# Softmax over 16,384 rows of 512: the two late loads go from GpSimd's DMA queue to SyncE's, between the stores

## The chip, the cores and the metric

The kernel runs on one core of a Trainium2 chip. The metric is the device time of one execution in microseconds (us), taken as the median of several runs. One further execution was profiled; every row of a profile below comes from such an execution.

## The reference

```python
x = randn(16, 1024, 512)  # float32
x_scaled = x / 2.0
x_max = max(x_scaled, axis=-1)
exp_x = exp(x_scaled - x_max)
out = exp_x / sum(exp_x, axis=-1)      # float32, same shape
```

It is a softmax over the last axis with a temperature of 2. There are 16,384 rows of 512 numbers: 33.55 MB are read and 33.55 MB written.

## The kernel before

The rows are dealt to the 128 partitions, so each partition has 128 rows of 512 numbers (2 KB each). They are cut into ten tiles of 3, 5, 15, 15, 15, 15, 15, 15, 15 and 15 rows per partition (`TILES`), numbered 0 to 9. A tile of 15 rows is 3,840 KB: 30 KB from each partition, which is one DMA packet of 30,720 bytes per partition and eight such packets for each of the 16 DMA engines.

On-chip memory holds 98 rows per partition (`arena`), so tiles 0 to 7 have places of their own, and tiles 8 and 9 reuse places: tile 8 lies over tiles 0, 1 and 2, and tile 9 over tiles 2 and 3. These two are the late loads (`LATE`). A late load may only be issued when the stores of what lies under it have landed: `s_home[8]` counts the landings of stores 0, 1 and 2, and `s_home[9]` counts that of store 3. (For tile 9 the wait for tile 8 has been passed already, which covers store 2.)

The work of each engine, in its own order:

- SyncE (SP) issues load 0 at the start and later all ten stores, in the order of the tiles (L214, L215). It waits first until tile 2 has been multiplied (`FIRST`), then issues stores 0, 1 and 2, and each further one as its tile's multiplies are done (`s_mul`, L138).
- ScalarE (ACT) issues loads 1 to 7 at the start, and then goes through the tiles row by row: one exponential of 512 numbers for each row, which also leaves the row's sum in `stats` (L206 and L274). Rows are counted in chunks of 5; before each chunk ACT takes a token (`s_go`, L142), which TensorE's queue hands on when the tile's load has landed. No maximum is subtracted.
- VectorE (DVE) takes 15 rows at a time (5 in the last tile): reciprocal of the sums (L168), then a multiply of the rows in place (L171).
- GpSimd (POOL) issues loads 8 and 9 (L178 to L181). It waits first until the exponentials have come to row 83 (`TURN`), and for each late load for its `s_home`. After that it clamps all sums for a test whether they are in a sound range (L182, once all exponentials are done).
- The test goes on over DVE (L186), a one-number matmul (L198) and a flag (L190). With the flag set, a slow version with the maximum, in the functions `vector`, `scalar` and `gpsimd`, is skipped, as it is with these data.
- SP waits at the end until the second-last store (`s_near`) and all others (`s_end`, L260) have landed.

DMAs of SP, ACT and GpSimd go into one queue each; the 16 DMA engines serve all three queues. The profile names them by number and tells the kinds apart: those of SP and ACT are `hardware_dynamic`, that of GpSimd is `software_dynamic`.

Of the kernel before, what the change touches and what calls it, by code (L numbers as in the profile page):

```python
# [13 lines left out]
LATE = {8: (0, 1, 2), 9: (3,)}  # L14
# [4 lines left out]

SPREAD = 1  # L20

TURN = 83

FIRST = 2

# [5 lines left out]
def kernel(  # L31
# [5 lines left out]
    nc = tc.nc  # L37
# [30 lines left out]
    def dram(ap, t):  # L68
        b, r, _ = tiles[t]
        return ap[b * P : (b + r) * P].rearrange("(p r) d -> p r d", r=r)  # L70

    def sb(t):
        _, r, at = tiles[t]
        return arena[:, at : at + r, :]
# [3 lines left out]
    starts = [sum(sizes[:k]) for k in range(len(sizes))]  # L78
# [15 lines left out]
    s_home = {t: nc.alloc_semaphore(f"s_home{t}") for t in LATE}  # L94
    s_near = nc.alloc_semaphore("s_near")
    s_end = nc.alloc_semaphore("s_end")
    s_exp = nc.alloc_semaphore("s_exp")
# [17 lines left out]
    def load(eng, t):  # L115
        r = tiles[t][1]
        parts = [(0, P, 0, r)]
        if t == SPREAD:
            parts = [(0, P, 0, r - 1), (0, 126, r - 1, r), (126, P, r - 1, r)]
        for p, q, lo, hi in parts:  # L120
            eng.dma_start(  # L121
                out=sb(t)[p:q, lo:hi], in_=dram(xf, t)[p:q, lo:hi]
            ).then_inc(ld[t], 16)
# [6 lines left out]
    def landings(ts):  # L130
        return 16 * len(list(ts))
# [5 lines left out]
    def store(eng, t):  # L137
        eng.wait_ge(s_mul, upto[t])  # L138
        eng.dma_start(out=dram(of, t), in_=sb(t)).then_inc(sem_of.get(t, s_end), 16)

    def take(eng, sem, n):
        eng.wait_ge(sem, n).then_inc(sem, -n)  # L142

    def rounds(eng, body):


        i = eng.alloc_register("general")
        eng.wait_ge(s_near, 16)
        eng.wait_ge(s_flag, 1)
        eng.reg_load(i, flag[0:1, 0:1])  # L150
        with eng.While(lambda: eng.snap(i, min_val=0, max_val=1) < 1):
            body()
            eng.reg_add(i, i, 1)
# [9 lines left out]
    def program():  # L163

        for j, ks in enumerate(pairs):
            b, c = starts[ks[0]], sum(sizes[k] for k in ks)
            a = b % ARENA
            nc.vector.reciprocal(  # L168
                out=recip[:, b : b + c], in_=stats[:, b : b + c]
            )._wait_ge(s_exp, ks[-1] + 1).then_inc(s_rec, 1)  # L170
            nc.vector.tensor_mul(  # L171
                out=arena[:, a : a + c],
                in0=arena[:, a : a + c],
                in1=recip[:, b : b + c].unsqueeze(2).to_broadcast([P, c, D]),
            )._wait_ge(s_rec, j + 1).then_inc(s_mul, 1)

        nc.gpsimd.memset(ones[:, :], 1.0).then_inc(s_ones, 1)  # L177
        nc.gpsimd.wait_ge(s_exp, starts.index(TURN))  # L178
        for t, us in LATE.items():
            nc.gpsimd.wait_ge(s_home[t], landings(us))  # L180
            load(nc.gpsimd, t)  # L181
        nc.gpsimd.tensor_scalar(  # L182
            out=inside[:, :], in0=stats[:, :], scalar1=LO, scalar2=HI,
            op0=Alu.max, op1=Alu.min,
        )._wait_ge(s_exp, len(sizes)).then_inc(s_cnt, 1)
        nc.vector.scalar_tensor_tensor(  # L186
            out=inside[:, :], in0=inside[:, :], scalar=1.0, in1=stats[:, :],
            op0=Alu.mult, op1=Alu.is_equal, accum_out=count[:, :],
        )._wait_ge(s_cnt, 1).then_inc(s_cnt, 1)
        nc.vector.tensor_scalar(  # L190
            out=flag[:, :], in0=total[:, :], scalar1=float(N), scalar2=None, op0=Alu.is_ge,
        )._wait_ge(s_tot, 1).then_inc(s_flag, 1)


        for t in range(len(tiles)):
            nc.tensor.wait_ge(ld[t], 48 if t == SPREAD else 16).then_inc(s_go, owner.count(t))
        nc.tensor.wait_ge(s_ones, 1)
        nc.tensor.matmul(  # L198
            total[:, :], lhsT=count[:, :], rhs=ones[:, :], start=True, stop=True
        )._wait_ge(s_cnt, 2).then_inc(s_tot, 1)  # L200

        nc.scalar.preload_act_table(Exp)  # L202
        for k, c in enumerate(HEAD):
            take(nc.scalar, s_go, 1)
            for b in range(starts[k], starts[k] + c):
                ins = nc.scalar.activation(  # L206
                    out=arena[:, b], in_=arena[:, b], func=Exp, scale=0.5,
                    accum_out=stats[:, b : b + 1],
                )
            ins.then_inc(s_exp, 1)  # L210
        exponentials(straight, n_rows)

        nc.sync.wait_ge(s_mul, upto[FIRST])
        for t in range(len(tiles)):  # L214
            store(nc.sync, t)  # L215

        x_g = xf.rearrange("(t p r) d -> t p r d", p=P, r=G)
        o_g = of.rearrange("(t p r) d -> t p r d", p=P, r=G)  # L220
        data = arena[:, 0:G]

        def vector():
            for i in range(n_rows // G):
                nc.vector.reduce_max(
                    out=g_max[:, :], in_=data, axis=mybir.AxisListType.X, negate=True
                )._wait_ge(g_go, i + 1).then_inc(g_top, 1)
                nc.vector.reduce_sum(
                    out=g_sum[:, :], in_=data, axis=mybir.AxisListType.X
                )._wait_ge(g_exp, i + 1).then_inc(g_add, 1)  # L230
                nc.vector.reciprocal(
                    out=g_sum[:, :], in_=g_sum[:, :]
                )._wait_ge(g_add, i + 1).then_inc(g_rec, 1)

        def scalar():
            for i in range(n_rows // G):
                nc.scalar.activation(out=data, in_=data, func=Exp, scale=0.5)._wait_ge(
                    g_sub, i + 1
                ).then_inc(g_exp, 1)

        def gpsimd():
            nc.gpsimd.wait_ge(s_end, at_end)
            for i in range(n_rows // G):
                nc.gpsimd.dma_start(out=data, in_=x_g[i]).then_inc(g_ld, 16)
                nc.gpsimd.wait_ge(g_ld, 16 * (i + 1)).then_inc(g_go, 1)
                nc.gpsimd.tensor_add(
                    out=data, in0=data, in1=g_max[:, :].unsqueeze(2).to_broadcast([P, G, D])
                )._wait_ge(g_top, i + 1).then_inc(g_sub, 1)
                nc.gpsimd.tensor_mul(
                    out=data, in0=data, in1=g_sum[:, :].unsqueeze(2).to_broadcast([P, G, D])  # L250
                )._wait_ge(g_rec, i + 1).then_inc(g_mul, 1)
                nc.gpsimd.wait_ge(g_mul, i + 1)
                nc.gpsimd.dma_start(out=o_g[i], in_=data).then_inc(g_st, 16)
                nc.gpsimd.wait_ge(g_st, 16 * (i + 1))

        rounds(nc.vector, vector)
        rounds(nc.scalar, scalar)
        rounds(nc.gpsimd, gpsimd)
        nc.sync.wait_ge(s_near, 16)
        nc.sync.wait_ge(s_end, at_end)  # L260

    def exponentials(first, end):
        row = nc.scalar.alloc_register(f"row{first}")
        nc.scalar.reg_mov(row, first)
        with nc.scalar.While(lambda: nc.scalar.snap(row, min_val=first, max_val=end) < end):
            now = nc.scalar.snap(row, min_val=first, max_val=end - E)
            take(nc.scalar, s_go, 1)
            at = nc.s_assert_within(
                now % ARENA, 0, ARENA - E,
                skip_runtime_bounds_check_because="no chunk reaches over the arena's end",  # L270
            )
            for r in range(E):
                data = arena[:, r : ARENA - E + 1 + r][:, bass.ds(at, 1)]
                ins = nc.scalar.activation(  # L274
                    out=data, in_=data, func=Exp, scale=0.5,
                    accum_out=stats[:, r : n_rows - E + 1 + r][:, bass.ds(now, 1)],
                )
            ins.then_inc(s_exp, 1)
            nc.scalar.reg_add(row, row, E)
# [12 lines left out]
    nc.switch_body(here, parent=None, valid_engines=[i.engine for i in jumps])  # L292
    loads()
    program()


# [28 lines left out]
```

## Time and profile before

| what | value |
|---|---|
| median of 3 runs | 159.78 us (159.69 to 159.83) |
| profiled execution, whole | 160.85 us |
| profiled execution, span of the page | 159.50 us |
| moved over the span | 67.11 MB, mean 421 GB/s |
| busy: DVE, ACT, POOL, PE | 73.2, 80.4, 2.2, 0.2 us |
| SP's issues: stores 0 to 2, 3, 4 | from 35.04, 44.2, 53.4 us |
| SP's issues: stores 5, 6, 7, 8, 9 | 63.57, 75.25, 91.18, 119.81, 132.57 us |
| GpSimd's issues: loads 8, 9 | 77.63, 89.73 us |
| ACT resumes for tiles 8, 9 | 102.02, 120.19 us |
| last landing (store 9) | 159.46 us |

The page counts an engine as busy only while it computes; issuing a DMA is no busy time for SP and ACT. Times are from the start of the span, which is SP's issue of load 0. The profiled execution is 1.07 us longer than the median of the runs without a profile. The lines of the profile on which the working rests stand in the prediction.

### The profile page before, as it was taken

What the parts mean: (1) busy time and instruction counts of PE and PEld (TensorE: products, weight loads), DVE (VectorE), ACT (ScalarE), POOL (GpSimd) and SP (SyncE); (2) the same over time, 40 slices, a digit from 0 to 9 for tenths busy, and PEclk for the clock granted to TensorE, in tenths of its full rate; (3) what the DMA queues carried; (4) which work ended last, traced back from release to release, by engine and by line L of the source; (5) the groups of instructions that cost most, each with busy time, mean ns of one, the idle gap of its engine ahead of it and who ended that gap; (6) DMA issues with size and microseconds to landing.
All of it is one profiled execution on the core that took longest, in us unless ns stands there. A gap on an engine that the chain in (4) does not pass through costs nothing. (4 is left out here: it accounts for less than half of the span.)

```text
span 159.5 us, 658 instructions
## 1 busy us (share of the span) xinstructions
PE 0.2 (0%) x2; PEld 0.1 (0%) x2; DVE 73.2 (46%) x27; ACT 80.4 (50%) x257; POOL 2.2 (1%) x8
## 2 busy tenths in 40 slices
PE   0000000000000000000000000000000000000000
PEld 0000000000000000000000000000000000000000
DVE  0047003989989599298029800000990993000000
ACT  0590699999979859705970000499008940000000
POOL 0000000000000000000100100000000010000000
DMA  7999999999999899999999999999999999999993
GB/s 276 411 455 401 462 408 455 408 455 393 444 461 443 344 434 465 401 462 408 455 424 439 416 447 431 431 447 416 455 408 470 393 470 393 462 401 470 393 470 154
DMA packets 3024, 67.11 MB, mean 421 GB/s; under 512 B 336, under 2 KB 336, under 8 KB 720
## 3 DMA queue, kind: packets, MB, share of 16 engines
q1 hardware_dynamic: 1584, 34.34, 50.2%
q10 hardware_dynamic: 1152, 24.90, 36.8%
q0 software_dynamic: 288, 7.86, 11.5%
HBM read 33.55 MB, written 33.55 MB: 421 GB/s over the span
## 5 line engine op out<-in xcount | busy, mean ns | idle before, releaser
L274 ACT ACTIVATE arena<-arena x125 | 76.6, 615 | 43.4 <-ACTq L142 43.4
L171 DVE TENSOR_TENSOR arena<-arena,recip 128x7680 f32<-128x7680 f32 (+2 forms) x12 | 70.2, 5846 | 0.4
L168 DVE RECIPROCAL recip<-stats 128x15 f32<-128x15 f32 (+2 forms) x12 | 2.7, 224 | 59.3 <-ACT arena L274 50.3
L274 ACT ACTIVATION_READ_ACCUMULATOR arena<-arena x125 | 23.4, 187 | 0.0
L202 ACT ACT_TABLE_LOAD x1 | 1.3, 1283 | 5.7 <-issue 5.7
L121 POOL DMA_DIRECT2D arena<-in_x_dram x2 | 1.3, 632 | 86.3 <-DMA out_dram<-arena 86.3
L206 ACT ACTIVATE arena<-arena 128x512 f32<-128x512 f32 x3 | 1.9, 618 | 0.0
L182 POOL TENSOR_SCALAR inside<-stats 128x128 f32<-128x128 f32 x1 | 0.6, 631 | 39.3 <-ACT arena L274 39.3
L206 ACT ACTIVATION_READ_ACCUMULATOR arena<-arena 128x1 f32 x3 | 0.6, 186 | 0.0
L198 PE MATMUL total<-ones,count 128*1 128x1 f32 x2 | 0.2, 164 | 132.8 <-DVE inside L186 132.8
L186 DVE SCALAR_TENSOR_TENSOR inside<-inside,stats 128x128 f32<-128x128 f32 x1 | 0.3, 285 | 0.0
L190 DVE TENSOR_SCALAR flag<-total 1x1 int32<-1x1 f32 x1 | 0.1, 146 | 0.3 <-PE total L198 0.3
L198 PEld LDWEIGHTS total<-ones,count 128*1 128x1 f32 x2 | 0.1, 80 | 132.8 <-DVE inside L186 132.8
L177 POOL MEMSET ones<- 128x1 f32 x1 | 0.1, 99 | 2.2 <-POOLq L39 2.2
L309 POOL MEMSET const-float32-0.0<- 128x1 f32 x1 | 0.1, 105 | 0.2 <-issue 0.2
L309 POOL MEMSET const-bfloat16-1.0<- 128x1 bf16 x1 | 0.1, 108 | 0.0
L309 POOL MEMSET const-uint8-127<- 128x1 uint8 x1 | 0.1, 108 | 0.0
L309 POOL MEMSET const-float32-1.0<- 128x1 f32 x1 | 0.1, 105 | 0.0
L186 DVE DVE_READ_ACCUMULATOR inside<-inside,stats 128x1 f32 x1 | 0.1, 84 | 0.0
## 6 DMA issues: line engine op xcount, KB each, us to landing
out_dram<-arena SPq DMA_DIRECT2D x8, 3840.0 KB, 47.7
arena<-in_x_dram ACTq DMA_DIRECT2D x6, 3840.0 KB, 36.5
arena<-in_x_dram POOLq DMA_DIRECT2D x2, 3840.0 KB, 27.1
out_dram<-arena SPq DMA_DIRECT2D x1, 1280.0 KB, 27.9
arena<-in_x_dram ACTq DMA_DIRECT2D x1, 1024.0 KB
arena<-in_x_dram SPq DMA_DIRECT2D x1, 768.0 KB, 5.6
out_dram<-arena SPq DMA_DIRECT2D x1, 768.0 KB, 15.2
arena<-in_x_dram ACTq DMA_DIRECT2D x1, 252.0 KB
```

The source lines that it names most:

```text
L121: eng.dma_start(out=sb(t)[p:q, lo:hi], in_=dram(xf, t)[p:q, lo:hi]).then_inc(ld[t], 16)
L168: nc.vector.reciprocal(out=recip[:, b : b + c], in_=stats[:, b : b + c])._wait_ge(s_exp, ks[-1] + 1).then_inc(s_rec, 1)
L171: nc.vector.tensor_mul(out=arena[:, a : a + c], in0=arena[:, a : a + c], in1=recip[:, b : b + c].unsqueeze(2).to_broadcast([P, c, D]),)._w ...
L177: nc.gpsimd.memset(ones[:, :], 1.0).then_inc(s_ones, 1)
L182: nc.gpsimd.tensor_scalar(out=inside[:, :], in0=stats[:, :], scalar1=LO, scalar2=HI, op0=Alu.max, op1=Alu.min,)._wait_ge(s_exp, len(sizes) ...
L186: nc.vector.scalar_tensor_tensor(out=inside[:, :], in0=inside[:, :], scalar=1.0, in1=stats[:, :], op0=Alu.mult, op1=Alu.is_equal, accum_ou ...
L190: nc.vector.tensor_scalar(out=flag[:, :], in0=total[:, :], scalar1=float(N), scalar2=None, op0=Alu.is_ge,)._wait_ge(s_tot, 1).then_inc(s_f ...
L198: nc.tensor.matmul(total[:, :], lhsT=count[:, :], rhs=ones[:, :], start=True, stop=True)._wait_ge(s_cnt, 2).then_inc(s_tot, 1)
L202: nc.scalar.preload_act_table(Exp)
L206: ins = nc.scalar.activation(out=arena[:, b], in_=arena[:, b], func=Exp, scale=0.5, accum_out=stats[:, b : b + 1],)
L274: ins = nc.scalar.activation(out=data, in_=data, func=Exp, scale=0.5, accum_out=stats[:, r : n_rows - E + 1 + r][:, bass.ds(now, 1)],)
L309: nc = _bacc.Bacc("TRN2", target_bir_lowering=False, num_devices=1)
```

## The change

GpSimd no longer issues the two late loads and no longer waits for row 83 or for the `s_home` semaphores. SP issues them in its chain of stores: load 8 after store 3 and ahead of store 4, and load 9 after store 4 and ahead of store 5, each after a wait for the same count of its `s_home` as before. Nothing else differs: the same transfers in the same sizes, the same places in `arena`, the same arithmetic.

```diff
-TURN = 83
+AHEAD = {4: 8, 5: 9}
...
         nc.gpsimd.memset(ones[:, :], 1.0).then_inc(s_ones, 1)
-        nc.gpsimd.wait_ge(s_exp, starts.index(TURN))
-        for t, us in LATE.items():
-            nc.gpsimd.wait_ge(s_home[t], landings(us))
-            load(nc.gpsimd, t)
         nc.gpsimd.tensor_scalar(
...
         nc.sync.wait_ge(s_mul, upto[FIRST])
         for t in range(len(tiles)):
+            if t in AHEAD:
+                late = AHEAD[t]
+                nc.sync.wait_ge(s_home[late], landings(LATE[late]))
+                load(nc.sync, late)
             store(nc.sync, t)
```

On SP's queue the order of the transfers becomes: load 0, stores 0, 1, 2, 3, load 8, store 4, load 9, stores 5, 6, 7, 8, 9.

## The prediction

> **What bounds the kernel now.** I read the slices and the DMA queues of the page first, then what the DMA queues' sequencer SP waits for, then the DMA traffic by stretches, then the last 4 us slice by slice, and last the packet records of the trace (start, duration, queue and bytes of each packet, which the views only sum).
>
> The page's slices and queues:
>
> ```profile
> DMA  7999999999999899999999999999999999999993
> ...
> q1 hardware_dynamic: 1584, 34.34, 50.2%
> q10 hardware_dynamic: 1152, 24.90, 36.8%
> q0 software_dynamic: 288, 7.86, 11.5%
> ```
>
> The 16 DMA engines are full from the second slice to the last but one, while DVE (46%) and ACT (50%) have free time. By size, q1 is SP's queue (all stores and load 0), q10 ACT's (loads 1 to 7) and q0 GpSimd's (loads 8 and 9, 7.86 MB). The chain of waits on the page ends with DVE's flag at 133.2 us, 26 us before the span does: it follows engines, and what ends last here is a transfer. SP's own waits say so:
>
> ```profile
> SPq L139 <- DVE arena L171: 118.2, 8, 28.3
> SPq L260 <- DMA out_dram<-arena: 26.5, 1, 26.5
> ```
>
> After its last issue SP waits 26.5 us (L260) for stores already queued. The stores have a backlog, so compute time and the order among transfers do not set the end; bytes per DMA engine, and time lost by one engine, do. The stretches:
>
> ```profile
> core 0: us, PE busy (x) PEld busy (x) DVE busy (x) ACT busy (x) POOL busy (x), PEclk, DMA share, GB/s
> 73.00:82.00 9.00, 0.00 (x0) 0.00 (x0) 2.22 (x1) 8.61 (x29) 0.73 (x1) 1.00 1.01 437
> ...
> 92.00:117.00 25.00, 0.00 (x0) 0.00 (x0) 5.62 (x2) 9.29 (x30) 0.00 (x0) 1.00 1.00 433
> 119.00:156.00 37.00, 0.19 (x2) 0.09 (x2) 10.18 (x10) 9.29 (x30) 0.63 (x1) 1.00 1.00 431
> ```
>
> SP's queue alone (73 to 82, 119 to 156) and SP's beside GpSimd's (92 to 117) move the same 431 to 437 GB/s. Last, DMA from 156 to 160 us in slices of 0.1 us:
>
> ```profile
> DMA  0079999077000000000700000000000000000000
> GB/s 0 0 307 922 1843 614 614 0 307 307 0 0 0 0 0 0 0 0 0 307 0 0 0 0 0 0 0 0 0 0 0 0 0 0 0 0 0 0 0 0
> ```
>
> A packet counts where it begins. Fifteen engines begin their last packet between 156.2 and 157.0; the single 307 in the slice at 157.9 is the last packet of one engine, late by itself. That engine sets the end. Call it A.
>
> A can be followed back packet by packet, each start on the end before it. Its completion for store 2 is at 76.65 us, against a median of 75.85 over the 16: 0.80 late. For store 9 it is at 159.11 against 157.57: 1.54 late. The added 0.74 is one packet. Nearly every 30,720-byte packet takes 1,138 ns on every queue; the one that A begins at 89.14 on q0 takes 1,875, 737 more. Of the 1,201 such packets that begin after 72 us only three take over 1,250 ns: this one, and two of another engine B (87.01 and 89.58 us; 1,441 and 1,516). All three are on GpSimd's queue. GpSimd issues load 9 meanwhile:
>
> ```profile
> 77.63 0.73 POOL L121 DMA_DIRECT2D arena<-in_x_dram  x1 [74.88 <-DMA out_dram<-arena]
> 89.73 0.54 POOL L121 DMA_DIRECT2D arena<-in_x_dram  x1 [11.37 <-DMA out_dram<-arena]
> ```
>
> A's and B's second long packets both contain 89.73 to 90.27. At the first issue (77.63) no q0 packet was moving yet, and none on q1 was slowed.
>
> **The change, part by part.** *Removed from GpSimd:* two issues (0.73 and 0.54 us) and their waits. GpSimd then waits for the last exponential (129.57 now), which is off the path: nothing gained.
>
> *Added to SP:* two waits and two issues of 0.33 to 0.44 us (the ten store issues; load 0's took 0.38). The first wait, for stores 0 to 2 landed, ends at 77.00 as before, since everything up to there is unchanged. Behind it stands store 4, which is issued at 53.4 now (end of its multiply) and would be at about 77.4 + 0.33. Behind the second, for store 3, stand stores 5 and 6. What covers both waits is the queue: at 77.0 store 3 has begun (its 8 packets per engine take 8 x 1.135 = 9.1 us), so it runs to 75.85 + 9.1 = 84.9, and load 8 is queued 7.5 us before that. From issue to first packet with full engines took 3.55 us (store 0: 35.04 to 38.59), so 4 us of cover remain; without the cover, that 3.55 would be a hole in the DMA stream. The second wait ends when A lands store 3, 85.7 + 0.35 = 86.1, with load 8 and store 4 still queued until 103: 17 us of cover. Both waits cost nothing.
>
> *Order of the transfers:* in one queue, at 9.1 us each: store 3 to 84.9, load 8 to 94.0, store 4 to 103.1, load 9 to 112.2, stores 5, 6, 7 to 139.4, store 8 to 148.5, store 9 to 157.6. Now, two queues share the engines packet by packet, and the loads land at 101.7 and 119.8; then at 95.2 and 113.3 (A's lag and 0.35 us added). Exponentials and multiplies follow sooner: store 8 is issued 18.1 us after its load lands now (101.7 to 119.8), so at 113.3, 26 us before its turn; store 9 12.8 us after (119.8 to 132.6), so at 126.1, 22 us before its turn. The queue does not run dry; these gains go nowhere.
>
> *Turns between reading and writing inside one queue* (store 3, load 8, store 4, load 9, store 5: four). The trace has none. Nearest row: A alternates a q1 store with a q0 load packet from 91 to 118 us, nearly every packet, with no gap and 1,138 ns each. Farthest: load 0 on idle engines, 0.63 us from the end of its issue (0.38) to its first packet (1.01). A gain is excluded, as neither queue has gaps. So 0 to 4 x 0.63 = 2.5 us; I take 0, since the near row is the same engine doing the same turns.
>
> *The long packets of q0.* They end with the queue, unless they belong to the moment instead. Bounds for the end: 0, and all of A's lag, 1.54. I take 0.74: from 119 to 156 us, SP's queue alone, no packet is over 1,250 ns. The other 0.80 of the lag stays, as it was there at 76.65; 0.60 of it is a packet of 1,738 ns at 61.3 on q10, beside q1. The Trainium skill (DMA: Bandwidth & Descriptors, "Latency and other measured facts") notes that DMA engines 7 and 15 are usually slower and guesses, for GpSimd's software path alone, at contention on the ports of its descriptor rings. The trace has two slow engines on q0 as it says, but A's lag of 61.3 us came without GpSimd; were the rule the whole of it, a hardware-only schedule would end at the median engine, and the sum would be 159.78 - 1.54 = 158.24.
>
> **Sum.** In the profiled execution (span 159.50, whole 160.85) A would end 0.74 earlier: span 158.76. The median of the runs is 159.78, 1.07 below the profiled whole; taking the same difference off it, 159.78 - 0.74 = 159.04, 0.46% less. From 0.2% (0.32 us) this kernel can be told from no change: its runs lie within 159.69 and 159.83.
>
> **Rivals.**
>
> *Same bytes, same time (0.23).* The delay at 89 us is of the moment: all but two engines had packets of 1.2 to 1.55 us at 54.5 without GpSimd, and A had its own at 61.3. Then A loses as much elsewhere, or the unprofiled runs never lost it. Against: q1 alone shows no such packet for 37 us. It gives 159.6 to 159.9, middle 159.78. The Trainium skill (same page, "Issuing engines are not separate DMA queues") has this as its rule: who issues changes only the issue time, as all queues run on the same 16 engines; by it the time stays at 159.78, and the 431 to 437 GB/s above agree with it.
>
> *Turns cost (0.14), slower.* Where SP's queue goes from a store to a load, the engine waits for the first bytes of the new read. Two turns at 0.63 us give 159.04 + 1.26 = 160.3, four give 161.6. Against: A's gapless alternation; for: there the packets came from two queues. It decides from (0.74 + 0.32)/4 = 0.27 us per turn.
>
> *The queue runs dry (0.05).* If load 8 reached the engines later than store 3's end, up to 3.55 us per wait would be lost: 159.04 + 3.55 = 162.6 for one. It needs 4 us more from issue to first packet than any SP issue here showed.
>
> That the change does not do what it says (loads later than now) would need a wait that ends later; both end at or before today's 77.0 and 89.4, and at 22 us of slack a late load shows in no time. I give it nothing of its own.
>
> **How the numbers follow.** The forecast has 0.58: 159.04, by itself 158.2 (all of A's lag gone) to 159.45. With the same-time case and the two-turn price the range is 158.2 to 160.3. Faster 0.58, same 0.23, slower 0.14 + 0.05 = 0.19.
>
> **What would show it.** Right: no q0; q1 1,872 packets and 42.2 MB; load 8 landed near 95 and load 9 near 113; ACT resuming near 95.5 and 113.6; SP's last issue near 126 and its wait at L260 about 32 us; no packet over 1,250 ns after 72 us; A about 0.8 behind the median at the end. A lag of 1.5 with the last store would show the second case; gaps or long packets between 85 and 112 us where load follows store the third; a dip in the DMA slices at 85 or 103 the fourth. A median over 159.46 makes the forecast wrong.

## The result, and the profile after

The changed kernel is slower: 161.49 us median of 6 runs (160.74 to 162.32), against 159.81 us for 6 runs of the kernel before beside them. The ratio is 1.0106, with a 95% interval of 1.0072 to 1.0140. Three later measurements, each in a batch of its own, put it at 1.0046 (1.0008 to 1.0083), 1.0049 (1.0018 to 1.0081) and 1.0046 (1.0007 to 1.0084). These ratios are of means. By the medians the changed kernel is slower by 1.68 us in the first batch and by 0.74, 0.27 and 0.30 us in the later ones: its six runs of the first batch were all over 160.7 us, while 16 of the 35 later ones were under 160.3. The sign held each time; the size depends on the batch, from 0.5 to 1.1% by the means.

The page after, slices and queues:

```profile
DMA  7998989899999899999999999999999999999994
...
q1 hardware_dynamic: 1872, 42.21, 61.9%
q10 hardware_dynamic: 1152, 24.90, 36.8%
```

GpSimd's queue is gone and its 288 packets are on q1. The DMA engines are as full as before. In the view by stretches (columns as in the prediction; the last two are the DMA share and GB/s):

```profile
73.00:82.00 9.00, 0.00 (x0) 0.00 (x0) 2.27 (x1) 8.47 (x27) 0.00 (x0) 1.00 1.01 437
...
119.00:156.00 37.00, 0.19 (x2) 0.09 (x2) 8.19 (x8) 4.85 (x16) 0.63 (x1) 1.00 1.01 435
```

The kernel before had 437 and 431 GB/s there. Over the whole stretch from 73 to 156 us it moved 432 GB/s and the changed kernel 430. SP's own waits:

```profile
SPq L139 <- DVE arena L171: 71.0, 5, 24.1
SPq L121 <- DMA out_dram<-arena: 40.1, 2, 31.9
SPq L260 <- DMA out_dram<-arena: 32.3, 1, 32.3
```

The second row is new, SP's two waits for landed stores. The third is the wait after the last issue: 32.3 us in place of 26.5. ACT's starts on the late tiles, in the timeline:

```profile
95.35 0.63 ACT L274 ACTIVATE arena<-arena  x1 [12.53 <-ACTq L142]
...
114.56 0.63 ACT L274 ACTIVATE arena<-arena  x1 [9.91 <-ACTq L142]
```

Both late loads land sooner than before (ACT resumed at 102.02 and 120.19 us there). So everything ahead of the last transfers got earlier or stayed, and the kernel got slower. The end, DMA from 156 to 161 us in slices of 0.125 us, a packet counted where it begins:

```profile
DMA  9559999559550000050000000000000000000000
GB/s 492 246 246 492 983 492 492 246 246 492 246 246 0 0 0 0 0 246 0 0 0 0 0 0 0 0 0 0 0 0 0 0 0 0 0 0 0 0 0 0
```

The same view of the kernel before:

```profile
DMA  0099955500000005000000000000000000000000
GB/s 0 0 983 1475 737 246 246 246 0 0 0 0 0 0 0 246 0 0 0 0 0 0 0 0 0 0 0 0 0 0 0 0 0 0 0 0 0 0 0 0
```

Before, 15 engines begin their last packets within 0.65 us, and one follows 1.05 us later. After, the 15 are spread over 0.97 us (the first slices hold packets before the last, too), and one follows 0.70 us later, at 158.1. By the packet records, the last engine ends 1.37 us behind the median of the 16 (157.89 and 159.26), and the median itself came 0.31 us later than before (157.58). How far the last engine is behind the median of the 16 when a transfer lands is called its lag below.

The records also show where that arose. After 72 us the changed kernel has 18 packets of 30,720 bytes over 1,250 ns, the kernel before three. Such packets are called long or stretched below. They stand in the late loads, above all in the last packets of load 8 (from 92.8 us) and of load 9 (from 110.8 us), up to 1,758 ns in place of 1,138. One can see it in the DMA view from 108 to 116 us (slices of 0.2 us). First the changed kernel's profile of 161.00 us, then its fourth one, of 160.00 us:

```profile
GB/s 154 154 154 922 768 461 0 154 307 1229 614 154 154 0 614 922 614 154 154 0 154 768 768 154 307 307 307 768 461 461 307 154 768 614 154 614 154 154 922 614
```

```profile
GB/s 0 0 0 1382 768 307 0 0 154 1690 461 154 0 0 614 1536 307 0 0 0 922 1229 307 0 0 0 1382 768 307 0 0 461 1536 307 154 0 0 922 1229 307
```

The engines begin their packets in a bunch every 1.13 us. In the second row the bunch stays narrow past load 9's end (about 112.2); in the first it frays from 111 us on and never closes again, since from there each engine has the same work left.

Those two profiles are of one kernel, and that is needed to read every number below: executions of one kernel differ in how late the last engine is. Over all batches, 77 of 115 runs of the kernel before were under 160.3 us, 33 between 160.3 and 161.0, and 5 over 161.0. Of the changed kernel 16 of 41 were under 160.3, 6 between, and 19 over 161.0. In all 18 profiles the whole time is 1.73 to 1.89 us more than the end of the last engine's last packet, so the time follows the last engine.

### The profile page after: what moved, and what is told of

The parts are those of the page before. It is cut to its first block, busy times and chain, and to the rows that moved or that the text cites. A ratio compares the mean times of both kernels' runs of the same rounds, so it can differ in the third digit from the quotient of the medians.

```text
span 159.6 us, 657 instructions
## 1 busy us (share of the span) xinstructions
PE 0.2 (0%) x2; PEld 0.1 (0%) x2; DVE 73.2 (46%) x27; ACT 80.4 (50%) x257; POOL 0.9 (1%) x6
## 2 busy tenths in 40 slices
DMA packets 3024, 67.11 MB, mean 420 GB/s; under 512 B 336, under 2 KB 336, under 8 KB 720
```

## The experiments

The theory was that turns, that is, changes from load to store or back inside SP's queue, stretch load packets, unevenly over the engines, and that the worst engine is the time. The rivals were that SP's queue is short at its new waits, that GpSimd's software queue suits the loads better than a hardware queue, that reading and writing in stretches is slower than side by side, and that chance made the difference. Since the runs scatter, the numbers below are means, each against the kernel before in the same batch. Batches ran on different chips, so differences are compared, not times.

**Does the packet that the prediction counted on come back?** The kernel before, once more:

> The kernel before, unchanged, for a second profile. If the 1,875 ns packet of GpSimd's queue at 89 us comes with every execution, it is there again, with a span near 159.5 us and a last engine 1.5 us behind the median. If it belonged to that one execution (the median of the runs, 159.8, less the 1.35 us outside the span would be a span of 158.4), the last engine is about 0.5 to 0.8 us behind and the span is near 158.4.

This execution took 160.54 us. The 1,875 ns packet was not there. One engine had three others on q0 (88.57, 93.56 and 107.35 us; 1,573, 1,314 and 1,520 ns) and ended 1.26 us behind the median. So that packet belonged to that one execution, but long packets on q0 as such did not. The two profiles of the kernel before, 160.85 and 160.54 us, are both from the upper third of its runs (median here 159.86).

**No turns: late loads on ACT's queue.**

```diff
-        nc.gpsimd.wait_ge(s_exp, starts.index(TURN))
-        for t, us in LATE.items():
-            nc.gpsimd.wait_ge(s_home[t], landings(us))
-            load(nc.gpsimd, t)
...
-        exponentials(straight, n_rows)
+        exponentials(straight, ARENA)
+        for t, us in LATE.items():
+            nc.scalar.wait_ge(s_home[t], landings(us))
+            load(nc.scalar, t)
+        exponentials(ARENA, n_rows)
```

> Late loads issued by ScalarE on its own hardware queue, when it is through with tile 7 (about 83 us) and store 3 has landed (about 89 us). Theory (turns): what costs is a queue that goes from load to store, which stretches the last packet of each late load by 0.05 to 0.6 us, another amount on each engine. With the loads in a queue of their own no queue turns: 159.5 to 160.0 us, like before, and no packet over 1.25 us at the ends of loads 8 and 9. Rival (hardware queues): late loads cost more when a hardware queue carries them: 161.0 to 162.0. Rival (short queue: at the waits SP's queue holds only what remains of store 3): here the stores are issued as before, so 159.8 too.

160.29 us mean against 159.95 (ratio 1.0023, 1.0004 to 1.0042): near the kernel before, well below the change's first 161.5. And beside the changed kernel in one batch:

> Late loads on ACT's hardware queue, beside the stores on SP's: no turns. Theory (turns): mean 0.5 us or more below the changed kernel, within 0.4 us of the kernel before. Rival (hardware queues are worse for late loads than GpSimd's): like the changed kernel.

160.24 against 160.04 before (ratio 1.0013, 0.9989 to 1.0037) and 160.61 for the changed kernel: 0.37 below the change where 0.5 was expected, and by itself within the scatter of these 11 and 11 runs (about 0.6 us either way). Over both batches one of 23 runs was over 161.0 us, of the changed kernel 19 of 41. That speaks against the hardware queue as the cost. But a late engine is found here too: in this profile (160.73 us) it ends 1.33 us behind the median, after long packets on q10 beside the stores.

**Two turns: both loads together, ahead of store 5.**

```diff
-AHEAD = {4: 8, 5: 9}
+AHEAD = {5: (8, 9)}
...
-            if t in AHEAD:
-                late = AHEAD[t]
+            for late in AHEAD.get(t, ()):
```

> Both late loads on SP's queue, one right behind the other, between store 4 and store 5: two turns in place of four, one of them from load to store (at the end of load 9). Theory (turns): half of the 1.7 us of the change or somewhat more, since the worst engine counts: 160.4 to 160.9 us; long packets at the end of load 9, none at the end of load 8. Rival (short queue): store 4 is issued early again, so the queue is as deep as before: 159.8. Rival (no mixing: reading and writing in stretches of their own is slower than side by side): the stretches are as long in sum, 161.5.

160.38 against 159.95 (1.0031, 1.0007 to 1.0056). The mean is just below what the theory gave (160.4 to 160.9), the median of 160.15 further below. The one profile fell on a run of 159.77 us; it has one long packet (1,518 ns at 96.3 us, early in load 8) and none at the end of load 9, where the theory had put them. Ahead of store 4 (`AHEAD = {4: (8, 9)}`), where SP's queue is short:

> Both late loads together ahead of store 4: two turns, and a short queue, since store 4 is only issued after store 3 has landed (about 86 us). Theory (turns): like the pair ahead of store 5, 159.9 to 160.5 us. Rival (short queue): like the change or slower, 161.0 to 162.0.

> Both late loads together ahead of store 4: two turns. Theory (turns): between the kernel before and the changed one, mean 0.4 to 1.0 us below the changed one; few runs over 161.0. Rival (short queue): like the changed one or slower.

160.26 against 160.36 (ratio 1.0000, 0.9971 to 1.0030), and 160.26 against 160.04 (1.0022, 0.9998 to 1.0047). With a short queue the pair is no slower than with a long one, and both times below the changed kernel (161.08 and 160.61 in the same batches; only the first of these differences is clear of the scatter). Its profiles, of 159.77 and 160.15 us, have five and four long packets at the end of load 9 (1,253 to 1,422 ns), and yet the last engine ends only 0.30 and 0.59 us behind the median. So long packets alone do not cost time; they do where they make the last engine later.

**Four turns, later: the long queue.**

```diff
-AHEAD = {4: 8, 5: 9}
+AHEAD = {5: 8, 6: 9}
```

> Load 8 ahead of store 5 and load 9 ahead of store 6, one place later than in the change. Store 4 is issued at 53.4 us again, so SP's queue holds stores 3 and 4 at the first wait and is never shorter than one whole store; the number of turns stays at four. Theory (turns): as slow as the change, 161.0 to 161.9 us, with stretched last packets of load 8 near 102 us and load 9 near 120 us. Rival (short queue): like before, 159.7 to 160.1.

160.71 against 160.36 (1.0031, 0.9990 to 1.0071, so not clear of no change), and 161.08 for the changed kernel there. Seven of 12 runs were at 159.92 to 160.05, five at 161.30 to 162.12. Five runs that late go against the short queue; seven at 160.0 go against the theory as it was worded, with 161.0 for all. In this kernel's profile ACT resumes for the late tiles at 104.23 and 122.64 us, later than in the kernel before, so the earlier landing of the loads in the change does not explain its late runs either.

**Four turns with smaller packets.** Each late load in parts of 8 and 7 rows:

```diff
+        if t in LATE:
+            parts = [(0, P, 0, 8), (0, P, 8, r)]
```

> Each late load in parts of 8 and 7 rows as in the kernel with eight turns, but the two parts of a load together: load 8 ahead of store 4, load 9 ahead of store 5, so four turns and the same packet sizes as with eight. Theory (turns): like the change, 161.0 to 161.9 us. Rival (more and smaller packets make the cost of the kernel with eight turns): like that one, 162.0 to 162.7.

160.80 against 160.36 (1.0025, 0.9989 to 1.0061): as the changed kernel or less.

**Eight turns: the same parts, each ahead of a store of its own.**

```diff
-AHEAD = {4: 8, 5: 9}
+AHEAD = {4: (8, 0), 5: (8, 1), 6: (9, 0), 7: (9, 1)}
```

> Each late load in two parts of 8 and 7 rows, with the four parts ahead of stores 4, 5, 6 and 7 on SP's queue: eight turns in place of four, four of them from load to store. Theory (turns): the cost of the change grows to 1.4 to 2 times: 162.2 to 163.2 us, and long packets stand at the ends of all four parts. Rival (short queue): the second wait and later stores are as covered as in the changed kernel: 161.5. Rival (no mixing): shorter stretches come closer to mixing: 161.0 to 161.5.

> Eight turns once more, beside four and sixteen on the same chip. Theory (turns): 1 us or more above the changed kernel, 161.8 to 162.8 us, with no run near 160. Rival (the five runs of the first time were chance): like the changed kernel.

162.36 against 159.95 and 161.87 against 160.16, both within what was expected; 11 runs, the lowest 161.04. That is 2.41 and 1.71 us above the kernel before. With the same packet sizes and four turns it was 0.44 us, in another batch, so the turns add more than a microsecond. Beside the changed kernel in the second batch (160.73) the 1.14 us are clear of the scatter. In the first profile the last engine is 0.23 us behind the median ahead of load 8, 0.84 after its first part, 1.27 after its second, and 2.26 at the end of load 9.

**Sixteen turns, and the same parts in four.** The late loads in parts of 4, 4, 4 and 3 rows, stores 4 and 5 in thirds, store 6 in halves. `ORDER` goes part by part, one of a load and one of a store, or puts all parts of load 8 ahead of store 4 and all of load 9 ahead of store 5:

```diff
+CUT = {8: (0, 4, 8, 12, 15), 9: (0, 4, 8, 12, 15), 4: (0, 5, 10, 15), 5: (0, 5, 10, 15), 6: (0, 8, 15)}
...
-        for t in range(len(tiles)):
+        for what, t, part in ORDER:
```

> Late loads in parts of 4, 4, 4 and 3 rows, stores 4 and 5 in thirds and store 6 in halves, one part of a load and one of a store in turn on SP's queue: sixteen turns in place of four. Theory (turns): slower than with eight, 163 to 166 us. Rival (no mixing: reading and writing in stretches is what costs): finer stretches come close to two queues side by side, 159.8 to 160.8.

> The same parts as with sixteen turns, but in the order of the change: all parts of load 8, of store 4, of load 9, of the later stores. Four turns, the same packet sizes. Theory (turns): like the changed kernel, mean 160.4 to 161.6 us. Rival (smaller packets cost): as with sixteen turns.

> The changed kernel, four turns, as the measure of this batch. Theory (turns): mean 0.3 to 1.7 us above the kernel before, runs from 159.9 to 162.3.

The means are 161.71 for sixteen turns, 161.23 for the same parts in four, 160.73 for the changed kernel and 160.16 for the kernel before. Finer interleaving did not bring SP's queue near two queues side by side, so the lack of mixing is not the cause. Nor did sixteen turns cost more than eight (161.87 here): the theory's 163 to 166 was wrong. Small parts may cost as well: with four turns each, 161.23 is 0.50 us over the changed kernel, and the sixteen turns are another 0.48 us over that, but neither step is clear of the scatter (about 0.7 and 0.6 us either way). The records show where the lag stops growing, not why. With sixteen turns it goes from 0.27 us at store 2 to 0.51 at store 3 and then by the parts of load 8 to 0.97, 1.63 and 2.22 us, and there it stays through all of load 9's turns. The step at store 3 is a store packet of 1,400 ns, the last ahead of load 8. With four it jumps from 1.06 to 2.33 at the end of load 8 and stays. In no profile did it end over 2.33. The tail with sixteen turns, again from 156 us in slices of 0.125:

```profile
DMA  5500059905050005000000000500000000000000
GB/s 246 246 0 0 0 246 983 2212 0 246 0 246 0 0 0 246 0 0 0 0 0 0 0 0 0 246 0 0 0 0 0 0 0 0 0 0 0 0 0 0
```

Fifteen engines begin their last packets within 0.7 us; the last one does so in the slice at 159.1, and ends 2.22 us behind the median, about two packets.

**The changed kernel again, and no late loads at all.**

> The changed kernel once more, beside the variants on one chip, and a second profile of it. Theory (turns): 161.0 to 161.9 us; the last packet of load 8 (near 93 us) and of load 9 (near 111 us) is stretched again on most engines, and the last engine is over 1.2 us behind the median at the end. If the stretched packets of the first profile were chance, they are missing here while the time is the same.

161.08 against 160.36; profile 161.02 us, last engine 1.60 behind. Its lag grows from 0.45 to 0.95 at the end of load 8 and to 1.60 at the end of load 9: the long packets are there again, but only on a few engines (five over 1,250 ns), not on most.

> The changed kernel beside the others of this batch: four turns on SP's queue. Theory (turns): the slowest of the batch, mean 161.0 to 161.6 us, with most runs over 160.5; stretched packets only in loads 8 and 9 after 72 us. Rival (chance of the batch): mean within 0.3 us of the kernel before.

160.61 against 160.04. This time the profile fell on a run of 159.90 us: no packet over 1,250 ns in the late loads, last engine 0.47 behind. Over its four profiles the changed kernel has 18, five, none and one long packets in the late loads at 161.00, 161.02, 159.90 and 160.00 us: time and stretch come and go together here. Six of its 11 runs were under 160.5, so "most over 160.5" was wrong.

> Left out: loads 8 and 9. Tiles 8 and 9 are computed on what lies in their place once the stores under it have landed; all ten stores stay. Loads 1 to 7 still run beside stores 0 to 2, but after 72 us only stores are in the queues. The time falls by 2 x 9.1 = 18.2 us, to 141.3 to 141.6. Theory (only load packets that have stores beside or behind them are stretched, and one late engine is the time): no run more than 0.3 us above the fastest, the last engine within 0.6 us of the median. Rival (late engines come from loads 5 to 7 beside stores 0 to 2, or from the stores): runs a whole microsecond above the fastest are as frequent as in the kernel before in this same batch.

```diff
-        for t, us in LATE.items():
-            nc.gpsimd.wait_ge(s_home[t], landings(us))
-            load(nc.gpsimd, t)
...
+            if t in LATE:
+                nc.tensor.wait_ge(s_home[t], landings(LATE[t])).then_inc(s_go, owner.count(t))
```

141.85 us mean of 5 runs, 141.65 to 142.31. The tail from 138 us in slices of 0.125:

```profile
DMA  5999090500000000000000000000000000000000
GB/s 246 737 1720 492 0 492 0 246 0 0 0 0 0 0 0 0 0 0 0 0 0 0 0 0 0 0 0 0 0 0 0 0 0 0 0 0 0 0 0 0
```

After 72 us, with only stores in the queues, no packet was over 1,250 ns and the last engine's lag stayed at 0.69 to 0.70 us from store 2 to the end. That lag had come with loads 5 to 7 beside stores 0 and 1 (1.98 us at store 1). One run was 0.66 above the fastest, twice what was expected, so the late loads are the larger source of lag but not the only one.

**All runs by the number of turns.** Runs over 161.0 us, a time that is rare in the kernel before:

| turns in SP's queue | kernels | runs over 161.0 us |
|---|---|---|
| none | kernel before; late loads on ACT's queue | 5 of 115; 1 of 23 |
| two | pair ahead of store 5; ahead of store 4 | 3 of 12; 3 of 24 |
| four | the change; later; in parts of 8 and 7; in four parts | 19 of 41; 5 of 12; 4 of 12; 5 of 12 |
| eight | parts of 8 and 7 rows | 11 of 11 |
| sixteen | parts of 3 to 8 rows | 5 of 6 |

The chips differ (four of the five late runs of the kernel before are of one batch), but the share rises with the turns up to eight.

## Why the prediction was wrong

- **"Long packets of q0" (-0.74 us) failed first.** The term was read from one packet of one execution and taken off the median of others. That execution was 160.85 us, the median 159.78, and two runs in three of the kernel before are under 160.3. The 1.07 us between the two was taken as a fixed difference between profile and runs. The records put it down to the late engine: every profile takes 1.73 to 1.89 us beyond the end of its last engine. No profile of the kernel before fell on a run near 159.8 us; in the six profiles of other kernels at 159.77 to 160.05 us the last engine is only 0.29 to 0.56 us behind the median. So at 159.8 us a gain of 0.74 was not there to be had. The rival "same time" had named this case ("the unprofiled runs never lost it").
- **"Turns" at 0 (of 0 to 2.5 us) failed second, and weighs more.** Of the 2.45 us between the forecast 159.04 and the measured 161.49, 0.77 is the gain that did not come and 1.68 the cost of the change, which this term had at nothing. The nearest row, one engine alternating a store and a load from two queues without a gap, did not carry over to one queue. With the change's four turns the mean rose by 0.57 to 1.70 us in four batches. The rival's mechanism was near and its place was wrong: it had the engine wait where a store gives way to a load. Most stretched packets of the change are the last of a load, ahead of a store, and the price is not per turn: it is what the engine that ends last has lost.
- **The range** left out the four-turn end, 161.6, though it was worked out.
- **Right: the bound.** The DMA engines stayed full and one late engine set the end.
- **Right: both waits are covered.** SP's queue never ran dry: by the packet records, on each engine a packet begins within 6 ns of the end of the one before, from 38 us to the end. ACT resumed at 95.35 and 114.56 us (95.5 and 113.6 forecast; the second is later by load 9's stretch), the last issue came at 126.96 (126), the wait at L260 was 32.3 us (32). The earlier landings went nowhere, as forecast.
- **Both rules of the Trainium skill (DMA: Bandwidth & Descriptors) fall short here.** "Issuing engines are not separate DMA queues" would have left the time alone; it rose by 0.5 to 1.1%, at the same 67.11 MB moved. "Latency and other measured facts" tentatively lays the slower engines 7 and 15 to GpSimd's software path. A slow last engine is here without that path: lags of 1.37 and 1.60 us in the changed kernel, and of 1.33 with ACT's queue. The records do not number the engines, so whether it is one of those two, as the prediction took A and B to be, is open.

What is shown: the time follows the last DMA engine; its lag arises almost wholly in load packets, mostly with stores beside or right behind them; the change makes such lag more frequent and larger (19 of 41 runs over 161.0 us, against 5 of 115); more turns in one queue raise it, up to eight. Not settled: why a load's packets are stretched there, why one engine takes most of it, why its lag stops near 2.3 us, and what decides from run to run. That the queue was short, that the loads landed too early, that reads and writes in stretches are slower as such, or that hardware queues are bad for loads, the runs speak against. No version here beat the kernel before; the ones nearest to it are ACT's queue and the pair ahead of store 4.

## What to carry to other kernels

Where the DMA engines are full to the end, read the last few microseconds engine by engine: the slowest engine is the time, not the mean rate. Before a term is sized from one profiled execution, see how that execution stands to the median, and take a second profile; a gap of 0.7% was the whole question here. In this kernel, loads that ran beside stores were better left in a queue of their own than put between the stores; where they shared one, they did better together than apart.

## What the runs showed of the hardware

- It is the load that yields. From 36 to 73 us, where SP's stores run beside ACT's loads, no store packet took over 1,155 ns in any of the 18 profiles, while 9 to 31 load packets in each took over 1,250. Either kind alone stays even: from 8 to 35 us, with loads only, the longest packet of all 18 profiles took 1,153 ns, and without the late loads no store packet after 72 us took over 1,250. Three store packets in all profiles did: the one of 1,400 ns above, and two of 1,254 and 1,260 ns with ACT's queue, each beginning where an instruction packet of 8 KB ended.
- One core's 16 DMA engines held 431 to 437 GB/s in stretches of 9 to 37 us, and the sum hardly cared whether two queues alternated or one ran alone (432 and 430 GB/s from 73 to 156 us in the two kernels). The difference between the kernels lies in how evenly the engines end.
- Two queues alternating on every packet cost less than one queue with four changes of direction: late loads on ACT's queue had a mean 0.20 to 0.34 us above the kernel before, the change 0.57 to 1.70. In the one batch that had both, the difference was within the scatter.
